# One tile of the weights' ring for the key and value rows of the window branch, in a one-core decoder layer on Trainium2

## Chip, cores and metric

The kernel runs on one core of one Trainium2 chip. The metric is the time of one execution in microseconds (us), by the median of repeated runs. Five engines have queues of their own: TensorE (PE, with its weight loads PEld), VectorE (DVE), ScalarE (ACT), GpSimd (POOL) and SyncE (SP). SP, ACT and POOL also issue the transfers between device memory and on-chip memory (DMAs). A name that ends in q, such as ACTq, is the sequencer of that engine when it issues a DMA.

## The reference

One layer of a decoder for 512 new prompt positions and 8 single new tokens, all in float32. The input projection has the columns of a state space group (u), of the queries, of three key and value branches (compressed, selected, sliding window) and of the gates:

```
proj = jnp.dot(h, lp['w_in'])
u, q, k_c, v_c, k_s, v_s, k_w, v_w, g = jnp.split(proj, offsets, axis=-1)
...
gates = jax.nn.sigmoid(g.astype(jnp.float32)).reshape(bsz, t, 3, N_HEADS)
o_ssm, s_last = ssm_mixer(u, ssm_s0, lp)
o_attn, win_state = attend(q, gates, kv_cmp, kv_slc, kv_win)
mix = jnp.concatenate([rmsnorm(o_ssm, ...), rmsnorm(o_attn, ...)], axis=-1)
x = x + gt1[:, None, :] * jnp.dot(mix, lp['w_out'])
...
x = x + gt2[:, None, :] * jnp.dot(jnp.square(jax.nn.relu(jnp.dot(h2, lp['w_up']))), lp['w_down'])
```

The key and value rows of the new positions (kv_cmp, kv_slc, kv_win) are outputs of their own.

## The kernel before, in words

Activations lie with the 1024 features on the partitions (8 blocks of 128) and 520 tokens along a row (512 prompt positions and 8 samples). Every float32 product is made of three matmuls: `split` (L65 to L67) makes a rounded copy on ACT (`wH` of weights, `hH` of activations) and the remainder on DVE (`wL`, `hL`), and the products hH·wH, hL·wH and hH·wL are added up in PSUM.

Weights come by DMA into `rawt(...)` tiles: one ring named `raw` of three buffers, 128 x 2048 float32 (1 MB) each, taken in turn by all weight loads of the layer (`wkv`, `wq`, `wglu` and others). A buffer can be filled again when the splits that read it are done.

`kv_proj(c)` does branch c (0 compressed, 1 selected, 2 window). It loads `wkv`, splits it in two halves, and goes over five token tiles t: four of 128 prompt positions and one of the 8 samples. A tile has 24 matmuls into a PSUM tile `pkv` (tag `pj`, two buffers; L660). For c of 1 and 2 ACT then copies the keys, each group twice, to `kvt` (L688) and the values to `Vx` (L690), stores both from ACT's own queue (L691 for the keys, L692 for the values), and PE transposes `kvt` into `pkt` (L695), from which `split` makes `KH` and `KL`. For c of 2 the gates come from the same PSUM tile (L117 on ACT, L118 on DVE). For t = 4 ACT copies `kvs` (L663). `kvt` is a tile of its own with two buffers, so that tile t takes the buffer of tile t - 2.

Behind each of the two `kv_proj` calls for c = 1 and 2 stands `state_space_outputs` for one of four feature blocks q (here q = 0 and 1): eight DMAs `yc`, four from SP and four from POOL (L903), bring scan results back from the scratch `yscr`, DVE adds them to `yf` (L905, L908) and `gelu` follows (`zt`, `uT`). `yc` has one buffer: the DMAs of block q wait for the `yf` of block q - 1. The next loop, for s = 0 and 1, loads 1 MB of query weights `wq` (L917), splits them (`wH<-wq`, `wL<-wq`), projects the queries with the matmuls `pj` (L619), and does blocks 2 and 3. Later loads of interest are three or four `rwin` (window rows of the samples, 1 MB each, L1165) and `wglu` (L1279).

The order on each engine isn't the order of the code: a scheduler with a simulated time line (`schedule_with_timeline_sim=True`) sets it, with waits on semaphores where tiles pass between engines. A DMA that SP or ACT issues gets one of eight completion semaphores (`DMAHW0` to `DMAHW7`), handed out in turn over the program, and before it is issued its engine waits for the DMA that had that semaphore before it. DMAs of POOL have eight of their own (`DMASW0` to `DMASW7`).

Of the kernel before, what the change touches and what calls it, by code (L numbers as in the profile page):

```python
# [10 lines left out]
F32 = mybir.dt.float32  # L11
# [6 lines left out]
P = 128  # L18
# [19 lines left out]
def body(tc, i, o, dbg=None):  # L38
# [19 lines left out]
    def pst(tag, name):  # L58
        if tag in bank.get("turns", ()):
            tag = next(bank["turns"][tag])  # L60
        return bank["tile"].tile([P, 512], F32, tag=tag, name=name, bufs=bank["tags"][tag])
# [3 lines left out]
    def split(h, l, src):  # L65
        nc.scalar.copy(h, src)  # L66
        nc.vector.tensor_tensor(l, src, h, ALU.subtract)  # L67
# [3 lines left out]
    def rawt(name):  # L71
        return raw.tile([P, 2048], F32, tag="raw", name=name)
# [42 lines left out]
    def sigmoid_(dst, src):  # L115

        nc.scalar.activation(dst, src, AF.Tanh, scale=0.5)  # L117
        nc.vector.tensor_scalar(dst, dst, 0.5, 0.5, op0=ALU.mult, op1=ALU.add)  # L118
# [61 lines left out]
    def whl(a, b):  # L180
        h = wp.tile([P, 1120], F32R, tag="wH", name="wH", bufs=2)[:, : a * b].rearrange("p (a b) -> p a b", a=a)
        l = wp.tile([P, 1120], F32R, tag="wL", name="wL", bufs=2)[:, : a * b].rearrange("p (a b) -> p a b", a=a)
        return h, l
# [422 lines left out]
    p1 = p1x.enter_context(tc.tile_pool(name="p1", bufs=1, side="right", reuse_waits="tile"))  # L606
# [30 lines left out]
    def kv_proj(c):  # L637
        c0 = 1024 + 256 * c
        r = rawt("wkv").rearrange("p (k c) -> p k c", k=KT)
        nc.sync.dma_start(r, i["w_in"][0, :, c0 : c0 + 256].rearrange("(k p) c -> p k c", p=P))  # L640
        nw = 280 if c == 2 else 256
        if c == 2:
            rg = p1.tile([P, KT, 24], F32, name="rg")
            nc.sync.dma_start(rg, i["w_in"][0, :, 1792:1816].rearrange("(k p) c -> p k c", p=P))
        ws = []
        for kk in range(2):
            kr = slice(4 * kk, 4 * kk + 4)
            h, l = whl(4, nw)
            split(h[:, :, 0:256], l[:, :, 0:256], r[:, kr])
            if c == 2:  # L650
                split(h[:, :, 256:280], l[:, :, 256:280], rg[:, kr])
            ws.append((h, l))
        for t in range(5):
            tok = slice(t * P, t * P + (P if t < 4 else NB))
            mp = P if t < 4 else NB
            ps = pst("pj", "pkv")
            for k in range(KT):
                wh, wl = ws[k // 4]
                for n, (x, w) in enumerate(((hH, wh), (hH, wl), (hL, wh))):
                    nc.tensor.matmul(ps[0:mp, 0:nw], x[:, k, tok], w[:, k % 4], start=(k == 0 and n == 0),  # L660
                                     stop=(k == KT - 1 and n == 2))
            if t == 4:
                nc.scalar.copy(kvs[:, c * 256 : (c + 1) * 256], ps[0:NB, 0:256])  # L663
                if c < 2:
                    nc.scalar.dma_start(o["new_%s_sample" % onames[c]], kvs[:, c * 256 : (c + 1) * 256])
                else:
                    nc.scalar.dma_start(o["new_win_sample"][:, T - 1], kvs[:, 512:768])
            else:
                kvt = p1.tile([P, 256], F32, tag="kvt", name="kvt", bufs=2)
                out = o["new_%s_prompt" % onames[c]][tok]  # L670
                if c == 0:
                    nc.scalar.copy(kvt, ps[:, 0:256])
                    nc.scalar.dma_start(out, kvt)
                    pk = pst("tr", "pkc")
                    for n in range(2):
                        nc.tensor.transpose(pk[:, n * P : (n + 1) * P], kvt[:, n * P : (n + 1) * P], ident)
                    for g in range(2):
                        for j2 in range(2):
                            for n in range(2):
                                nc.vector.tensor_copy(  # L680
                                    xTp[j2 * 64 : j2 * 64 + 64, n, g, :, t * 8 : t * 8 + 8],
                                    pk[g * 64 : g * 64 + 64, n * P : (n + 1) * P].rearrange(
                                        "p (c jp j2) -> p j2 jp c", c=8, j2=2)[:, j2])
                else:
                    br = c - 1

                    kv2 = kvt.rearrange("p (g a d) -> p g a d", g=2, a=2)
                    nc.scalar.copy(kv2, ps[:, 0:P].rearrange("p (g d) -> p g d", g=2).unsqueeze(2).to_broadcast([P, 2, 2, HD]))  # L688
                    vt = Vx[:, t, 2 * br : 2 * br + 2]
                    nc.scalar.copy(vt, ps[:, P:256].rearrange("p (g d) -> p g d", g=2))  # L690
                    nc.scalar.dma_start(out[:, 0:P].rearrange("t (g d) -> t g d", g=2), kv2[:, :, 0])  # L691
                    nc.scalar.dma_start(out[:, P:256].rearrange("t (g d) -> t g d", g=2), vt)  # L692
                    pk = pst("tr", "pkt")
                    for g in range(2):
                        nc.tensor.transpose(pk[:, g * P : (g + 1) * P], kvt[:, g * P : (g + 1) * P], ident)  # L695
                    split(KH[:, 2 * br : 2 * br + 2, tok], KL[:, 2 * br : 2 * br + 2, tok],
                          pk[:, 0:256].rearrange("p (g t) -> p g t", g=2))
            if c == 2:
                sigmoid_(gates[0:mp, t], ps[0:mp, 256:280])
    kv_proj(0)  # L700
    ada(4, "ad")

# [37 lines left out]
    for qd in range(NG // GQ):  # L740
# [89 lines left out]
        for g in range(GQ):  # L830
            c = slice(g * 80, (g + 1) * 80)
# [80 lines left out]
    for c in (1, 2):  # L912
        kv_proj(c)
        state_space_outputs((c - 1,))
# [715 lines left out]
```

## Time and profile before

| | |
|---|---|
| timed runs | 898.96, 900.66, 900.21 us, median 900.21 us |
| the profiled execution | 896.71 us, with a span of 895.0 us |
| granted TensorE clock, mean | 0.987 of full speed |
| PE busy | 845.8 us, 94% |
| PEld, DVE, ACT, POOL busy | 751.8, 519.8, 389.9, 64.0 us |

The span goes from the first to the last instruction that the profiler recorded; 1.7 us of the execution lie outside it. All rows below are from this one execution. Times of rows count from the start of the span.

### The profile page before, as it was taken

Reading aid. Unit: us, or ns where it says so; the run is one execution under the profiler, and the core shown is the slowest. Engines: PE = TensorE matmul, PEld = TensorE weight load, DVE = VectorE, ACT = ScalarE, POOL = GpSimd, SP = SyncE. Lnnn points to the kernel's source line nnn. Section 1 sums busy time; section 2 is a strip of 40 time slices with the busy share of each in tenths; the row PEclk is TensorE's granted clock in tenths of the full one; section 3 lists DMA queues with packets and bytes.
Section 4 is the critical chain, followed back from the end, with each engine's and each line's share of the span. In section 5 each row is a group of like instructions: output and inputs, shape, how many; then the busy total and the mean of one; then the engine's idle time right before and its main releaser. Section 6 shows DMA issues by size and latency. Waiting matters only on the chain.

```text
span 895.0 us, 16400 instructions
## 1 busy us (share of the span) xinstructions
PE 845.8 (94%) x6527; PEld 751.8 (84%) x6527; DVE 519.8 (58%) x1365; ACT 389.9 (44%) x883; POOL 64.0 (7%) x147
## 2 busy tenths in 40 slices
PE   2799998999998999998989999999999999999996
PEld 1557997888987766756679989999999999999996
DVE  5876666785766466668667874442333444434533
ACT  1555317453435466556655554442111344433322
POOL 6001201000152100000000000000000000000000
PEclk9999998999999999999989999999999999999998
DMA  8957577473773441203266553333333333232302
GB/s 290 319 195 247 181 157 193 138 247 116 203 244 92 165 166 64 77 2 142 73 210 198 180 190 94 94 96 94 95 95 95 94 95 92 82 86 75 92 1 96
DMA packets 111836, 122.36 MB, mean 137 GB/s; under 512 B 24500, under 2 KB 91880, under 8 KB 109584
## 3 DMA queue, kind: packets, MB, share of 16 engines
q1 hardware_dynamic: 101968, 88.66, 32.8%
q0 software_dynamic: 5488, 29.99, 9.6%
q10 hardware_dynamic: 4304, 2.66, 1.1%
q8 instruction: 51, 0.84, 0.4%
q14 instruction: 25, 0.20, 0.1%
HBM read 112.47 MB, written 13.03 MB: 140 GB/s over the span
## 4 chain that ended last, share of the span: by engine, by line
PE 66%; DVE 2%; ACT 1%; issue 0%; ACTq 0%; DVEq 0%
PE pup L1427 21%; PE pdn L1427 21%; PE pwo L1427 5%; PE pj L619 3%; PE po L1268 2%; PE ptp L1261 2%; PE pg L1289 2%; PE pS L1047 2%; PE pst L1232 1%; PE pkT L1038 1%; PE pst L1233 1%; PE psc L1174 1%; PE pstat L879 1%; PE poS L1136 0%; PE po L1349 0%; PE pst L1234 0%
## 5 line engine op out<-in xcount | busy, mean ns | idle before, releaser
L1427 PE MATMUL pdn<-hidH,wL 128*128 128x256 f32 (+1 forms) x480 | 136.0, 283 | 0.0
L1427 PE MATMUL pdn<-hidL,wH 128*128 128x256 f32 (+1 forms) x480 | 135.8, 283 | 0.0
L1427 PE MATMUL pup<-h2L,wH 128*128 128x256 f32 (+1 forms) x480 | 135.5, 283 | 0.0
L1427 PE MATMUL pdn<-hidH,wH 128*128 128x256 f32 (+1 forms) x480 | 135.3, 282 | 0.0
L1427 PE MATMUL pup<-h2H,wL 128*128 128x256 f32 (+1 forms) x480 | 135.0, 282 | 0.0
L1427 PE MATMUL pup<-h2H,wH 128*128 128x256 f32 (+1 forms) x480 | 134.5, 283 | 0.0
L1427 PEld LDWEIGHTS pup<-h2L,wH 128*128 128x128 f32 x480 | 90.4, 188 | 0.8 <-DVE rs L105 0.8
L1427 PEld LDWEIGHTS pup<-h2H,wH 128*128 128x128 f32 x480 | 89.8, 188 | 0.8 <-ACT h2H L66 0.8
L1427 PEld LDWEIGHTS pdn<-hidH,wL 128*128 128x128 f32 x480 | 90.4, 188 | 0.0
L1427 PEld LDWEIGHTS pdn<-hidL,wH 128*128 128x128 f32 x480 | 90.2, 188 | 0.1
L1427 PEld LDWEIGHTS pup<-h2H,wL 128*128 128x128 f32 x480 | 90.3, 188 | 0.0
L1427 PEld LDWEIGHTS pdn<-hidH,wH 128*128 128x128 f32 x480 | 90.3, 188 | 0.0
L66 ACT CAST wH<-wdn 128x1024 fp32r<-128x1024 f32 x30 | 31.5, 1049 | 114.2 <-PE pdn L1427 104.3
L67 DVE TENSOR_TENSOR wL<-wup,wH 128x1024 fp32r<-128x1024 f32 x30 | 36.7, 1225 | 57.9 <-ACT wH L66 57.9
L67 DVE TENSOR_TENSOR wL<-wdn,wH 128x1024 fp32r<-128x1024 f32 x30 | 36.8, 1225 | 54.3 <-ACT wH L66 54.3
L401 PE MATMUL ph<-xc,w 128*128 128x256 f32 (+2 forms) x320 | 62.9, 346 | 0.7 <-DVE xc L391 0.7
L401 PEld LDWEIGHTS ph<-xc,w 128*128 128x128 f32 x320 | 50.8, 194 | 11.0 <-issue 5.4
L66 ACT CAST wH<-wup 128x1024 fp32r<-128x1024 f32 x30 | 31.5, 1050 | 47.3 <-PE pup L1427 37.5
L1507 ACT ACTIVATE rl<-pup 128x256 f32<-128x256 f32 (+1 forms) x64 | 24.5, 385 | 45.5 <-PE pup L1427 45.4
L389 ACT COPY xc<-pxc 64x256 f32<-64x256 f32 x96 | 32.1, 366 | 22.5 <-DVE xc L391 18.8
L1508 DVE TENSOR_TENSOR rl<-rl 128x256 f32<-128x256 f32 (+1 forms) x64 | 27.2, 426 | 22.9 <-ACT rl L1507 22.9
L1436 DVE SCALAR_TENSOR_TENSOR xT<-pdn,mod,xT 128x256 f32<-128x256 f32 x32 | 15.2, 478 | 41.7 <-PE pdn L1427 41.6
(569 smaller groups left out, 2038.8 us busy)
## 6 DMA issues: line engine op xcount, KB each, us to landing
wada<-w_ada SPq DMA_DIRECT2D x20, 1024.0 KB, 5.1
wup<-w_up SPq DMA_DIRECT2D x16, 1024.0 KB, 5.4
wdn<-w_down SPq DMA_DIRECT2D x16, 1024.0 KB, 5.7
wo<-w_out SPq DMA_DIRECT2D x8, 1024.0 KB, 5.5
wada<-w_ada SPq DMA_DIRECT2D x8, 512.0 KB, 16.0
rwin<-state_win SPq DMA_DIRECT2D x4, 1024.0 KB
new_win_sample<-state_win POOLq DMA_DIRECT2D x2, 2044.0 KB, 8.6
wkv<-w_in SPq DMA_DIRECT2D x3, 1024.0 KB, 8.1
```

Of the source, the lines that this page charges most:

```text
L66: nc.scalar.copy(h, src)
L67: nc.vector.tensor_tensor(l, src, h, ALU.subtract)
L389: nc.scalar.copy(dst[:, :, :, hf], srcv[:, :, :, hf])
L401: nc.tensor.matmul(phv[:, lo:hi, 0:w], w1[n][:, r_], xc[n][:, lo:hi, r_ % 8, off : off + w], start=(r_ == 0), stop=(r_ == 15))
L619: nc.tensor.matmul(ps[:, 0:HB], w[:, k], x[:, k, hc], start=(k == 0 and n == 0), stop=(k == KT - 1 and n == 2))
L1047: nc.tensor.matmul(S[b4 * 32 : b4 * 32 + 32], q4[:, 4 * grp + b4], kts[b4], start=True, stop=True)
L1261: nc.tensor.transpose(pt_[:, c : c + P], at(qt, kt * P, P), ident)
L1268: mm = nc.tensor.matmul(po[hh * 64 : hh * 64 + 64, kt * P : T], Vx[:, kt, kb], PT[:, c0 : c0 + T - kt * P], start=(br == 0 and kt == 0), s ...
L1289: nc.tensor.matmul(ps[:, 0:HB], r[:, k, c], zf[k][:, hc], start=(k == 0), stop=(k == 3))
L1427: nc.tensor.matmul(ps[:, 0 : b - a], w, x[:, a:b], start=first and n == 0, stop=last and n == 2)
L1507: nc.scalar.activation(rl, ps[:, 0 : b - a], AF.Relu)
L1508: nc.vector.tensor_tensor(rl, rl, rl, ALU.mult)
```

## The change

For the window branch (c = 2) `kv_proj` takes one more tile of the weights' ring, `kvr`, behind the splits of the weights, and token tile t uses its columns 256t to 256t + 255 as `kvt`. For the other branches nothing changes. From here on a line of the code stands two lines lower (L688 becomes L690, L691 and L692 become L693 and L694, L903 becomes L905, L917 becomes L919).

```diff
@@ -650,6 +650,8 @@
             if c == 2:
                 split(h[:, :, 256:280], l[:, :, 256:280], rg[:, kr])
             ws.append((h, l))
+
+        kvr = rawt("kvt") if c == 2 else None
         for t in range(5):
             tok = slice(t * P, t * P + (P if t < 4 else NB))
             mp = P if t < 4 else NB
@@ -666,7 +668,7 @@
                 else:
                     nc.scalar.dma_start(o["new_win_sample"][:, T - 1], kvs[:, 512:768])
             else:
-                kvt = p1.tile([P, 256], F32, tag="kvt", name="kvt", bufs=2)
+                kvt = kvr[:, t * 256 : (t + 1) * 256] if c == 2 else p1.tile([P, 256], F32, tag="kvt", name="kvt", bufs=2)
                 out = o["new_%s_prompt" % onames[c]][tok]
                 if c == 0:
                     nc.scalar.copy(kvt, ps[:, 0:256])
```

The ring then goes round in the order wkv (c = 1), wkv (c = 2), kvr, wq, wq, wglu instead of wkv, wkv, wq, wq, wglu. The second `wq` so takes the buffer of the second `wkv`, where it took that of the first, and `wglu` takes that of `kvr`. The scheduler also sets another order in several places.

On ACT, in the window branch, these were the rows from the copy of tile 2 to the first cast of query weights. In brackets is what an instruction waits for; `Activation` and `PE` are those engines.

```order
L688 COPY kvt<-pkv 128x256 [waits DMAHW1_49,PE_49]
L690 COPY Vx<-pkv 128x128
L117 ACTIVATE gates<-pkv 128x24
L691 DMA new_win_prompt<-kvt 128x2x64 [waits DMAHW0_49,Activation_49]
L692 DMA new_win_prompt<-Vx 128x128 [waits Activation_49]
L688 COPY kvt<-pkv 128x256 [waits DMAHW3_49,PE_49]
L690 COPY Vx<-pkv 128x128
L117 ACTIVATE gates<-pkv 128x24
L66 CAST KH<-pkt 128x2x128 [waits PE_49]
L691 DMA new_win_prompt<-kvt 128x2x64 [waits DMAHW2_49,Activation_49]
L692 DMA new_win_prompt<-Vx 128x128 [waits DMAHW4_49,Activation_49]
L66 CAST wH<-wq 128x1024 [waits PE_49]
```

In the changed kernel this stands on ACT from the second store of tile 1 to the first store of tile 3; the second store of tile 3 (L694) and the cast `wH<-wq` are the next two rows.

```order
L694 DMA new_win_prompt<-Vx 128x128 [waits DMAHW7_49,Activation_49]
L690 COPY kvt<-pkv 128x256 [waits PE_49]
L692 COPY Vx<-pkv 128x128
L117 ACTIVATE gates<-pkv 128x24
L66 CAST KH<-pkt 128x2x128 [waits PE_49]
L693 DMA new_win_prompt<-kvt 128x2x64 [waits DMAHW0_49,Activation_49]
L694 DMA new_win_prompt<-Vx 128x128 [waits DMAHW1_49,Activation_49]
L66 CAST KH<-pkt 128x2x128 [waits PE_49]
L690 COPY kvt<-pkv 128x256 [waits PE_49]
L692 COPY Vx<-pkv 128x128
L117 ACTIVATE gates<-pkv 128x24
L693 DMA new_win_prompt<-kvt 128x2x64 [waits DMAHW3_49,Activation_49]
```

The two copies `kvt` lost their waits for a DMA; before, those were the stores of tiles 0 and 1. The second store of tile 1 and the first store of tile 2 now wait for the semaphores 7 and 0, which by the turn of the program were last given to the two `wq` loads.

On SP, at the place where the selected branch begins, these were the rows (`mscr`, `Tz` and `yscr` belong to the state space scan):

```order
L785 DMA mscr<-M_2385 128x64 [waits DVE_49]
L835 DMA yscr<-ys 128x320 [waits DMAHW3_49,Activation_49]
L917 DMA wq<-w_in 128x8x256 [waits DMAHW4_49,PE_49]
L917 DMA wq<-w_in 128x8x256 [waits DMAHW6_49,PE_49]
L787 DMA Tz<-mscr 128x8x64 [waits DMAHW7_49,DMAHW2_49]
L785 DMA mscr<-M_2487 128x64 [waits DVE_49]
```

In the changed kernel SP has the `wq` loads behind the last `yscr` and the first `yc` of block 3:

```order
L837 DMA yscr<-ys 128x320 [waits DMAHW5_49,Activation_49]
L905 DMA yc<-yscr 16x8x80 [waits DMAHW0_49,DMAHW1_49,DMASW5_49,DMAHW2_49,DMASW4_49,DMAHW3_49,DMASW3_49,DMAHW6_49,DMASW2_49,DVE_49]
L919 DMA wq<-w_in 128x8x256 [waits DMAHW7_49]
L919 DMA wq<-w_in 128x8x256
L905 DMA yc<-yscr 16x8x80
L905 DMA yc<-yscr 16x8x80 [waits DMAHW5_49,DMAHW4_49]
L905 DMA yc<-yscr 16x8x80
L1167 DMA rwin<-state_win 128x2x1024 [waits DMAHW2_49,PE_49]
L1167 DMA rwin<-state_win 128x2x1024 [waits DMASW3_49,DMASW6_49,DMASW2_49,DMASW7_49,DMASW1_49,DMAHW4_49,DMASW0_49,PE_49]
L1167 DMA rwin<-state_win 128x2x1024 [waits DMAHW6_49]
L1281 DMA wglu<-ssm_w_glu 128x4x512 [waits DMAHW1_49,DMAHW0_49,DMAHW3_49,PE_49,Activation_49]
```

The two loads of the query weights moved behind thirteen `yc`, both `Tz` and all `yscr`, and are issued once the `yf` of block 2 is done, for which the `yc` ahead of them waits. `wglu`, which stood ahead of the `rwin` loads, now stands behind three of them.

## Rows read from the trace of the kernel before

**Rows 1.** Page, busy time of each engine and its share of the span.

```profile
PE 845.8 (94%) x6527; PEld 751.8 (84%) x6527; DVE 519.8 (58%) x1365; ACT 389.9 (44%) x883; POOL 64.0 (7%) x147
```

**Rows 2.** Waits, 252 to 280 us: who waits for whom, total, times, longest.

```profile
ACT kvt L688 <- DMA new_win_prompt<-kvt: 6.2, 2, 3.4
...
PE pj L619 <- ACT wH L66: 1.3, 1, 1.3
...
PE pkt L695 <- ACT kvt L688: 1.1, 2, 0.7
...
PE pkv L660 <- DVE wL L67: 0.5, 1, 0.5
```

**Rows 3.** Timeline of ACT, window branch: start, duration, instruction, idle time before it.

```profile
259.13 0.39 ACTq L691 DMA_DIRECT2D new_win_prompt<-kvt  x1
...
266.68 0.37 ACT L688 COPY kvt<-pkv 128x256 f32<-128x256 f32 x1 [2.87 <-DMA new_win_prompt<-kvt]
...
267.08 0.39 ACTq L691 DMA_DIRECT2D new_win_prompt<-kvt  x1
...
267.51 0.48 ACTq L692 DMA_DIRECT2D new_win_prompt<-Vx  x1
270.67 0.37 ACT L688 COPY kvt<-pkv 128x256 f32<-128x256 f32 x1 [3.35 <-DMA new_win_prompt<-kvt]
```

**Rows 4.** Timeline of PE, window branch to the first query projection.

```profile
252.52 0.32 PE L660 MATMUL pkv<-wH,hL 128*8 128x256 f32 x1
...
266.48 0.29 PE L660 MATMUL pkv<-wH,hL 128*128 128x280 f32 x1
267.11 0.44 PE L695 MATMUL pkt<-ident,kvt 128*128 128x128 f32 x2 [0.34 <-ACT kvt L688]
...
270.06 0.29 PE L660 MATMUL pkv<-wH,hH 128*8 128x280 f32 x1
...
273.12 0.39 PE L619 MATMUL pj<-hH,wH 128*128 128x260 f32 x1 [1.33 <-ACT wH L66]
...
274.73 0.42 PE L619 MATMUL pj<-hH,wL 128*128 128x260 f32 x1
...
277.98 0.30 PE L619 MATMUL pj<-hH,wL 128*128 128x260 f32 x1
278.12 0.28 PE L619 MATMUL pj<-hH,wH 128*128 128x260 f32 x1
...
278.60 0.28 PE L619 MATMUL pj<-hL,wH 128*128 128x260 f32 x1
```

**Rows 5.** Windows: stretch, length, engines' busy time (instructions), granted clock, DMA share, GB/s.

```profile
234.00:239.00 5.00, 5.00 (x45) 5.00 (x44) 1.82 (x7) 1.39 (x5) 0.16 (x2) 1.00 1.16 319
275.00:278.00 3.00, 3.00 (x16) 3.00 (x16) 2.85 (x5) 0.78 (x2) 0.91 (x1) 0.50 0.03 7
410.00:420.00 10.00, 8.40 (x52) 5.46 (x52) 8.88 (x24) 8.08 (x24) 0.00 (x0) 1.00 0.56 227
450.00:470.00 20.00, 18.23 (x117) 15.87 (x116) 12.33 (x39) 11.04 (x25) 0.00 (x0) 0.83 0.55 188
```

**Rows 6.** Timeline of SP: the query weights, and the loads in the window branch.

```profile
226.93 1.76 SPq L917 DMA_DIRECT2D wq<-w_in  x2
...
256.46 2.89 SPq L1165 DMA_DIRECT2D rwin<-state_win  x3
270.67 1.96 SPq L903 DMA_DIRECT2D yc<-yscr  x4
```

**Rows 7.** Timeline of ACT, selected branch.

```profile
238.58 0.35 ACTq L692 DMA_DIRECT2D new_slc_prompt<-Vx  x1
238.97 0.37 ACT L66 CAST KH<-pkt 128x256 fp32r<-128x256 f32 x1 [3.59 <-DMA wq<-w_in]
```

**Rows 8.** Timeline of DVE, window branch.

```profile
256.74 0.70 DVE L127 TENSOR_TENSOR uT<-zt,yf 128x520 f32<-128x520 f32 x1
...
267.75 1.12 DVE L905 SCALAR_TENSOR_TENSOR yf<-uT,vec,yc 128x512 f32<-128x512 f32 x1 [0.22 <-DMA new_win_prompt<-Vx]
```

**Rows 9.** Page, DMA issues: times, KB each, median us from issue to landing.

```profile
wup<-w_up SPq DMA_DIRECT2D x16, 1024.0 KB, 5.4
...
wada<-w_ada SPq DMA_DIRECT2D x8, 512.0 KB, 16.0
```

## The prediction, made before the result was known

> **What bounds the kernel now.** I read the busy times first: PE works 94% of the span [rows 1], so a change can save only where PE stands still or runs slowly, and what it saves there reaches the end if PE stays the bound behind it. Then I looked at the waits of the stretch that the diff touches. Three of them are PE's and hang together: PE waits 1.1 us in two pieces for the copies `kvt`, and 1.3 us for the cast of the first query weights, while ACT itself waits 6.2 us in two pieces for the stores of earlier `kvt` tiles; 0.5 us more PE waits for the second split of the window weights [rows 2]. The timeline of ACT gives the reason. The store of tile 0 is issued at 259.13, and the copy of tile 2, which takes its buffer, starts at 266.68; that of tile 3 starts at 270.67, 3.35 us of it waiting for the store of tile 1 [rows 3]. Both stores are 64 KB and lie in flight beside `rwin` loads of 1 MB each, issued from 256.46 [rows 6]. On PE the reader is to see that matmuls run without a gap until 266.48, and that the first query matmul stands at 273.12 [rows 4]. Last I read the granted clock: from 275 to 278 it is 0.50, the 1.2 GHz level, although PE is busy all the time there [rows 5]. It fell behind this cluster of gaps and came back at 278.
>
> What lies between is counted so. At 266.48 PE still has one matmul under way (0.13 us), then a pair of transposes, 24 matmuls and another pair. From 267.11 to 270.06 the first pair and 22 matmuls take 2.95 us to the start of the last of them [rows 4]; one of the steps is 0.13 us, so the whole rest is 2.95 + 3 x 0.13 + 0.26 = 3.6 us. It could end at 266.61 + 3.6 = 270.2, and the query matmuls begin 2.9 us later than that. Behind them come 15 matmuls from 274.73 to 277.98, 0.217 us apart; from 278.12 to 278.60 four steps take 0.12 us each [rows 4]. The low clock costs 15 x (0.217 - 0.12) = 1.4 us.
>
> **The change part by part.** *The buffers.* Four `kvt` tiles get four places, so the two waits of ACT for stores, 2.87 and 3.35 us [rows 3], are gone from the program; the rows of ACT in the new order show the copies waiting for PE alone. Without any other wait PE would reach the query matmuls at 270.2 instead of 273.12, and 0.47 us earlier still if the wait for the second split went too: 269.7.
>
> *The loads of the query weights.* In the old order SP issues both `wq` at 226.93 [rows 6], 40 us ahead of need. In the new one they stand behind the `yf` of block 2. I place that so: on DVE the `uT` ahead of it ends at 256.74 + 0.70 = 257.4 in the old order, and a `yf` takes 1.12 us and a short second part, 0.2 [rows 8], which makes 258.7. That chain begins with the copy of the samples' rows on ACT, which needs the matmul at 252.52; before, this matmul stood behind the seven small scan products, and now it stands ahead of them, which gives it up to 0.9 us. So the `yf` ends at 257.8. One `yc` of 1.96/4 = 0.5 us is issued first [rows 6], so that the first `wq` is issued at 258.3.
>
> The trace has no load of `wq` under these conditions. Its nearest row for one load of the same size and shape is `wup`, 5.4 us from issue to landing [rows 9]. For the second I add the time to move 1.05 MB at the 319 GB/s that ran when the old `wq` loads ended [rows 5]: 3.3 us. The second lands at 258.3 + 5.4 + 3.3 = 267.0. The bounds are 265.3 (`yf` 0.7 us earlier and a rate of 410 in place of 319, which saves 0.7 more, and a little off the first) and, above, the row of eight queued `wada` loads, 16.0 us from issue to landing [rows 9]: 274.3.
>
> *The new wait.* ACT's first store of tile 2 waits for the semaphore that the second `wq` holds. Behind it in ACT's queue stand one more store, a cast `KH`, the copies of tile 3 with gates, two stores and the cast `wH<-wq`, and PE's last transposes and all query matmuls wait for these. Their time from the rows: stores 0.39 and 0.48 [rows 3], a cast 0.37 [rows 7], and from the copy of tile 3 to the first query matmul 273.12 - 270.67 = 2.45 [rows 3, 4]; together 3.7 us. With the second `wq` at 267.0 the query matmuls begin at 270.7, and 269.7 is their floor. The gain up to there is 273.12 - 270.7 = 2.4 us. Each us by which `wq` is later costs one; at 273.12 - 3.7 = 269.4 nothing is left.
>
> That ACT can be held so, the trace shows already: in the selected branch a store waited 3.59 us for a `wq` load and was issued at 238.58 [rows 7]. There nothing of it reached PE, which was busy 5.00 of the 5 us [rows 5]. That wait goes, since the loads moved; it was covered and gives nothing.
>
> *The clock.* The cluster of three gaps before 274 shrinks to one of about 1 us ahead of the query matmuls, and the short ones for `wL` and `kvs` behind it, which stay. Elsewhere PE was busy 8.40 of 10 us at a clock of 1.00, from 410 to 420 [rows 5], while 18.23 of 20 us from 450 to 470 went with 0.83 [rows 5]. So gaps of such a size decide it either way. I take the clock as kept: 1.4 us gained; the other bound is nothing.
>
> *What else moves.* On POOL, the `yc` of block 2 now stand ahead of the stores of the scan's states, which nobody in the kernel reads. `rwin` comes up to 4 us later, and its first reader is 40 us away. In the attention stage, 400 to 470 us, products are ordered anew. I find no term there that points one way; the stretch 450 to 470 has 1.8 us of idle PE [rows 5], and I take this as the size of what a new order can give or take, with nothing in the middle.
>
> **Sum.** 2.4 + 1.4 + 0 = 3.8 us. The profiled execution of 896.71 us becomes 892.9, and its span of 895.0 becomes 891.2. The median of the timed runs lies 3.5 us above the profiled execution; from it the same gain makes 900.2 - 3.8 = **896.4 us**. About 0.2%, 1.8 us, is what a measurement of this kernel can tell from no change.
>
> **What speaks against it.** The store of tile 0, 64 KB, needed 7.5 us from issue until its buffer was taken again, and that of tile 1 some 10 us [rows 3], beside the three `rwin` loads [rows 6]. The Trainium skill, page "DMA: Bandwidth & Descriptors", section "Queues, rings and completion order", says that a DMA engine takes turns between the queues that have work for it, and that the write which signals completion lands only behind all earlier writes of that engine, over all its queues. The stores of the trace agree with the second half, at 7.5 us for 64 KB. By that rule the `wq` signal would come behind whatever small stores and `yc` transfers went ahead, so somewhat later than my sum has it, and the stores of tiles 0, for which tiles 2 and 3 wait too, would come with it.
>
> **Rivals.**
>
> *The wait only changes its name.* ACT waits for `wq` as long as it waited for the stores. For it: the first `wq` goes out 1.8 us later than the first `rwin` did before [rows 6], and two `rwin` follow closely. Against it: 2 MB stand ahead of the signal, where the store that held tile 3 had three `rwin` of 1 MB ahead of it [rows 3, 6]. It takes a second `wq` at 268.5 to 270.5, a gain of 0.9 to a loss of 1.1, with the clock falling as before: 899.3 to 901.3, say 900.2.
>
> *Slower.* The same wait, but with the two `rwin` loads taking their share of the engines before `wq` is complete. 4.2 MB at the 319 GB/s of the old `wq` loads [rows 5] take 13.2 us, and 2.1 us of start (5.4 less 3.3) come ahead of it: the second `wq` lands at 258.3 + 15.3 = 273.6, near the 16.0 us of the `wada` row. The query matmuls begin at 277.3, and the time is 900.2 + 4.2 = 904.4. It decides for slower from a `wq` at 269.4 + 1.8 = 271.2. Against it: all these loads come from SP, in this order. The same page of the Trainium skill speaks of turns between queues, not between loads of one queue, and has descriptors of one queue consumed in order; no run so far shows the two loads apart.
>
> *Half the gain.* The copies come early, but the clock falls all the same, or the new order of the attention stage takes back 1.8 us: 2.4 us of gain in the first case, 2.0 in the second, 898.
>
> That the change doesn't do what it says can be left out, since the order shows the copies without their waits.
>
> **How the numbers follow.** The forecast, a gain of 3 to 5.5 us (up to 3.4 at the floor of 269.7, 1.4 of the clock, and a little of the attention stage), has 0.48: 894.7 to 897.2 is its own range. Half the gain 0.18, the wait that changes its name 0.22, slower 0.12. Faster by over 0.2%, so below 898.4, is the forecast and most of half the gain: 0.65. Within 0.2% is the third case with the rest: 0.23. Slower is 0.12. The range has to leave out no more than 2 in 10: from 894.4, a little below the forecast's own, to 901.0, which leaves out the slower case and the top of the third.
>
> **What the profile of the changed kernel would show.** Right: no copy `kvt` of the window branch waits for a DMA; ACT's first store of tile 2 is issued near 267, released by `wq`; PE begins the query matmuls near 270.7 with one gap of about 1 us ahead; the granted clock stays at 1.00 from 270 to 280; all later stages are shifted by the same 3 to 4 us. Wrong, if the first `wq` is issued much behind 258.3 (the `yf` of block 2 late), if its landing takes over 11 us (the other two cases), if the clock row of 275 to 278 comes back, or if PE's idle time between 400 and 470 us grows from what it was by over 1.8 us.

## The result: 893.8 us, and where it lies in the profile after

The changed kernel took 894.54, 893.93, 893.70 and 892.50 us, median 893.82 us. The kernel before, with one more run beside it, has a median of 899.59 us. The ratio is 0.9934, with a 95% interval of 0.9916 to 0.9952: faster by 5.8 us, where 3.8 us were forecast, and 0.6 us below the range. Of the runs further down one of e9, 1375.5 us at a mean clock of 0.563, is left out of its median.

The profiled execution of the changed kernel took 894.54 us, so that the two profiled executions differ by 2.2 us only. This is the first thing to understand, and most of the runs below serve it. The page of the changed kernel, span and busy times of the engines (for [rows 1]):

```profile
span 892.8 us, 16399 instructions
...
PE 847.5 (95%) x6527; PEld 753.3 (84%) x6527; DVE 521.7 (58%) x1365; ACT 389.8 (44%) x883; POOL 64.8 (7%) x147
```

Its waits from 252 to 280 us, in the form of [rows 2]:

```profile
ACT kvt L690 <- DMA wq<-w_in: 2.6, 1, 2.6
...
PE pj L619 <- ACT wH L66: 1.2, 1, 1.2
...
PE pj L619 <- DVE wL L67: 0.2, 1, 0.2
```

The waits for stores are gone, PE's two waits for `kvt` and the one ahead of the second split too. What is left is one wait of PE for the cast of the query weights, and one of ACT for a `wq` load. It reads as a wait of the copy `kvt`; the timeline of ACT shows that it is the store ahead of it (for [rows 3]):

```profile
261.09 0.39 ACTq L693 DMA_DIRECT2D new_win_prompt<-kvt  x1
...
264.03 0.34 ACTq L694 DMA_DIRECT2D new_win_prompt<-Vx  x1
264.41 0.37 ACT L690 COPY kvt<-pkv 128x256 f32<-128x256 f32 x1 [2.57 <-DMA wq<-w_in]
...
264.92 0.39 ACT L66 CAST KH<-pkt 128x256 fp32r<-128x256 f32 x1
267.73 0.39 ACTq L693 DMA_DIRECT2D new_win_prompt<-kvt  x1
...
268.95 0.38 ACT L690 COPY kvt<-pkv 128x256 f32<-128x256 f32 x1
...
270.43 1.04 ACT L66 CAST wH<-wq 128x1024 fp32r<-128x1024 f32 x1 [0.84 <-PE pkt L697]
```

The second store of tile 1 is issued at 264.03 and the first store of tile 2 at 267.73, each after a stop of ACT's sequencer: by the order these two wait for the two `wq` loads. SP issued those at 257.01 (for [rows 6]):

```profile
257.01 1.74 SPq L919 DMA_DIRECT2D wq<-w_in  x2
258.80 2.49 SPq L905 DMA_DIRECT2D yc<-yscr  x3
267.91 1.59 SPq L1167 DMA_DIRECT2D rwin<-state_win  x3
```

On PE the window branch begins at 253.35 and the query products at 271.52, against 252.68 (the table below) and 273.12 [rows 4]. So this execution came 0.7 us later to the branch, and took 18.17 us from its first product to the first query product, before 20.44.

```profile
253.35 0.51 PE L662 MATMUL pkv<-wH,hH 128*128 128x280 f32 x2
...
271.52 0.39 PE L619 MATMUL pj<-hH,wH 128*128 128x260 f32 x1 [1.20 <-ACT wH L66]
```

The windows behind (for the second of [rows 5]; columns as there) show the clock down here too, for about as long, only earlier:

```profile
271.00:275.00 4.00, 3.30 (x16) 2.95 (x17) 3.72 (x9) 2.55 (x6) 0.71 (x1) 0.75 1.04 405
275.00:278.00 3.00, 3.00 (x21) 3.00 (x21) 0.79 (x3) 0.73 (x3) 0.34 (x1) 0.76 1.06 407
```

### The profile page after: what moved, and what is told of

Its sections match the earlier page's. It is cut to its first block, busy times and chain, and to the rows that moved or that the text cites. A ratio compares the mean times of both kernels' runs of the same rounds, so it can differ in the third digit from the quotient of the medians.

```text
span 892.8 us, 16399 instructions
## 1 busy us (share of the span) xinstructions
PE 847.5 (95%) x6527; PEld 753.3 (84%) x6527; DVE 521.7 (58%) x1365; ACT 389.8 (44%) x883; POOL 64.8 (7%) x147
## 4 chain that ended last, share of the span: by engine, by line
PE 62%; issue 4%; DMA 2%; ACT 1%; DVE 1%; ACTq 0%; DVEq 0%; POOLq 0%
PE pup L1429 21%; PE pdn L1429 21%; PE pwo L1429 5%; PE pj L619 3%; PE pg L1291 2%; PE ptp L1263 1%; PE po L1270 1%; DMA xT<-xscr 1%; PE pS L1049 1%; PE pst L1234 1%; PE pkT L1040 1%; PE pst L1235 1%; PE psc L1176 1%; PE pstat L881 1%; PE poS L1138 0%
## 5 line engine op out<-in xcount | busy, mean ns | idle before, releaser
L1244 ACT ACTIVATE pe<-pst,mxa 128x512 f32<-128x512 f32 (+1 forms) x64 | 33.4, 529 | 16.9 <-DVE mxa L1240 15.5
```

What stands on the lines that cost most here:

```text
L1244: nc.scalar.activation(at(qt, 0, nk), d, AF.Exp, bias=mx[:, qt : qt + 1], accum_out=dn[:, qt : qt + 1])
```

## Experiments

**More traces of both kernels** (no edit). Executions of one kernel differ here by up to 7 us, so one pair of traces says little of 5 us.

e1, the kernel before in five rounds:

> The kernel before, unchanged, to learn how its executions differ. The timed runs moved by 5.8 us, the two profiled executions only by 2.2 us. Theory A: the first profiled execution of before (896.7 us) was a short one and the usual one is near 899.6, with one more stretch at half clock or a longer one somewhere; then this ratio is 1.000 within 0.002, the times lie at 898 to 901, and a second trace shows half-clock stretches that add up to 1 to 3 us more than before's. Theory B: the timed runs of before were the odd ones; then this one lies at 896 to 897.5.

e2, the changed kernel in five rounds:

> The changed kernel, unchanged. Theory A: a ratio of 0.993 to 0.995 again, 893 to 895 us. Theory B: 0.997, 896 to 897. In both the query projection begins 2.4 us earlier against the start of the window branch than before, with ACT's first store of tile 2 released by the second load of query weights.

Measured: e1 had 898.94 us (895.87 to 902.41), a ratio to the kernel before of 0.9995 [0.9976, 1.0013]; e2 had 894.47 (893.15 to 896.18), 0.9934 [0.9913, 0.9955]. Theory A holds for the times: the first profiled execution of before, 896.71, was a short one. The trace of e1 has one more fall of the clock than the first, 3.4 us long, from 37 to 41 us, long before the window branch.

Then single executions, for traces:

> The kernel before once more, for a trace of a usual execution: the runs of it so far lie at 895.7 to 902.4 with mean clocks of 0.987 to 0.981, and both traces in hand are from the better end (0.987 and 0.985). If the timed gain of 5 to 6 us, beyond the 2.9 us that the stages show, is a matter of the clock, a trace at 0.983 or 0.981 shows one or two more half-clock stretches than the first, each costing about 1.5 us, and the same waits. If it isn't, such a trace shows a longer wait or transfer somewhere.

> As e6: one more execution of the kernel before. The stretch from the window branch's first product to the first query product takes 20.4 to 20.9 us whatever the clock does elsewhere; what differs from trace to trace is the number and place of half-clock stretches.

> The changed kernel once more: 18.0 to 18.2 us from the window branch's first product to the first query product, and one half-clock stretch of 3.4 us behind it. If the changed kernel has fewer half-clock stretches as a rule, its mean clock is 0.985 to 0.987 again where before's are 0.981 to 0.985.

> One more execution of the kernel before, for a trace with a mean clock of 0.983 or less, as 29 of 56 runs of it had. If the usual execution differs from the traces in hand by the clock alone, its waits and its stretch of 20.4 to 20.9 us are the same, and it has one or two half-clock stretches more, each 3.4 us long and worth about 1.6 us.

> The kernel before once more, like the run ahead of it: a trace with a mean clock of 0.983 or less is wanted. Its waits in the window branch and its stretch of 20.4 to 20.9 us should be the same, with one or two half-clock stretches of 3.4 us more than in the first trace.

> The kernel before once more. From the window branch's first product to the end the six traces of it take 641.9 to 642.9 us, three traces of the changed kernel 639.2 to 639.5. If the rest of the timed gain (5.1 us of medians against 2.9 us of this) comes from chance ahead of the window branch, the start of that branch here is anywhere from 252.5 to 257 and the part behind it 642 to 643 again. If before has executions in which the part behind is longer (a second half-clock stretch in the window branch or in the attention stage), it is 644 or more in some of these looks.

> The kernel before once more, with the two theories of the run ahead of it: the part behind the window branch's first product takes 642 to 643 us in every execution and the rest is the time ahead of it, or it takes 644 us or more in some of them, with a half-clock stretch that the first traces lack.

> The changed kernel once more. Chance ahead of the window branch: that branch starts at 252.5 to 257 as in before, and 639 to 640 us follow. If the two kernels differ ahead of it, though their instructions are the same up to 225 us, the start stays at 253 to 255 in all looks at the changed kernel while before's goes to 256 or more.

> The changed kernel once more, with the theories of the run ahead of it: a start of the window branch anywhere from 252.5 to 257 and 639 to 640 us behind it, or a start that stays at 253 to 255.

The table has, for each execution with a trace, the start of the window branch (first product with 280 columns), the time from there to the first query product, from there to the first `psc` (the product behind the first half of the query products), from there to the end of the span, the mean granted clock and the time. All in us, from the timelines of PE.

| execution | start | to queries | to psc | rest | clock | time |
|---|---|---|---|---|---|---|
| before, first | 252.68 | 20.44 | 14.21 | 607.7 | 0.987 | 896.71 |
| e1 | 254.12 | 20.93 | 14.16 | 607.4 | 0.985 | 898.33 |
| e6 | 253.01 | 20.47 | 14.05 | 607.4 | 0.987 | 896.58 |
| e7 | 254.27 | 20.58 | 14.17 | 607.5 | 0.985 | 898.21 |
| e12 | 253.66 | 21.39 | 12.67 | 608.3 | 0.985 | 897.73 |
| e13 | 256.84 | 21.23 | 14.18 | 607.5 | 0.983 | 901.37 |
| e14 | 254.65 | 21.06 | 12.67 | 608.4 | 0.983 | 898.52 |
| e15 | 253.79 | 21.15 | 15.47 | 608.8 | 0.982 | 900.91 |
| changed, first | 253.35 | 18.17 | 14.00 | 607.3 | 0.985 | 894.54 |
| e2 | 255.00 | 17.98 | 14.02 | 607.5 | 0.985 | 896.18 |
| e8 | 252.88 | 18.20 | 12.47 | 608.5 | 0.987 | 893.80 |
| e16 | 253.98 | 18.06 | 12.47 | 608.4 | 0.985 | 894.62 |
| e17 | 254.59 | 17.98 | 12.48 | 608.0 | 0.985 | 894.85 |

The means are 20.91, 13.95 and 607.9 before, 18.08, 13.09 and 607.9 after: 2.8 us of stall, 0.9 us in the query products, nothing in the rest. To the query products the two kernels don't overlap. Not all of the expectations held: four of before's executions took longer than the expected 20.4 to 20.9 us to the query products, and e8 lacks the low clock that was expected behind them. From the start of the branch to the end of the span e15 took 645.4 us, the sign of the second theory of e14 and e15; the other seven of before took 641.9 to 642.9, the five of the changed kernel 638.5 to 639.5.

The second column goes with the clock: e8, e16 and e17 kept it. The windows of e8 that answer to those shown above:

```profile
271.00:275.00 4.00, 3.75 (x27) 3.39 (x28) 3.88 (x8) 2.11 (x6) 1.05 (x1) 1.00 1.04 408
275.00:278.00 3.00, 3.00 (x28) 3.00 (x27) 1.95 (x5) 2.06 (x6) 0.00 (x0) 1.00 1.08 403
```

But of the 1.5 us that the clock gives back there about 0.9 are taken again later. Wherever the query products kept the clock, in e8, e16 and e17 as in e12 and e14 of before, the clock fell at 408 to 420, in the attention stage, and the rest took 608.0 to 608.5 us; in seven of the other eight it didn't fall there, and the rest took 607.3 to 607.7. The same window in the first trace of the changed kernel and then in e8:

```profile
405.00:420.00 15.00, 12.18 (x76) 8.10 (x76) 14.23 (x37) 9.76 (x27) 1.25 (x2) 1.00 0.55 210
...
405.00:420.00 15.00, 12.56 (x60) 8.90 (x60) 12.51 (x32) 11.09 (x31) 0.00 (x0) 0.77 0.45 179
```

The other end is e15, an execution of the kernel before in which the branch and the query products take 36.6 us, against 30.5 in e17. Its windows:

```profile
254.00:258.00 4.00, 3.41 (x16) 3.33 (x16) 3.93 (x9) 2.31 (x5) 4.00 (x7) 0.63 0.50 132
...
275.00:282.00 7.00, 6.45 (x30) 6.22 (x31) 4.67 (x8) 2.80 (x7) 1.05 (x1) 0.54 0.28 53
```

Here the clock fell twice: at 254, around the wait for the second split of the window weights, 0.59 us in this trace, and again behind the gaps at 275, for twice as long as in the first trace. All eight traces of before have the low clock somewhere in this stretch, of the changed kernel two of five. Added up over windows of 1 us from the start of the branch to 480 us, the time at 1.2 GHz is 10.1 to 10.2 us in all five traces of the changed kernel and in five of before; e12 and e14 have 13.6 and e15 20.3. What these three have more begins with a fall at 254 or 255, behind PE's wait for the second split, a wait that the changed kernel lacks. So the falls differ from execution to execution; that the changed kernel has fewer of them here rests on three traces of eight against none of five.

The start of the branch differs by up to 4.2 us between executions of before, with the low clock more or less often ahead of it; the means, 254.1 before and 254.0 after, are the same, as they should be with the same order of instructions up to about 225 us.

**e3: four buffers, loads early.** Before, with four buffers from a small pool for the window branch:

```diff
-                kvt = p1.tile([P, 256], F32, tag="kvt", name="kvt", bufs=2)
+                kvt = kw.tile([P, 256], F32, tag="kvw", name="kvt", bufs=4) if c == 2 else p1.tile([P, 256], F32, tag="kvt", name="kvt", bufs=2)
...
+    kwx = ExitStack()
+    kw = kwx.enter_context(tc.tile_pool(name="kw", bufs=1, reuse_waits="tile"))
     for c in (1, 2):
...
```

> Before, with four buffers for kvt in the window branch from a pool of its own; the ring keeps its old order, so the query weights are loaded early as before. If the gain comes from the buffers alone, the copies of tiles 2 and 3 follow PE, the query matmuls begin near 270.0 (before 273.1, changed kernel 271.5 or 270.7 when its later start is taken off), and the time is 1 us or more below the changed kernel's. If ACT's stores then wait for other loads (wglu and rwin stand on the semaphores), the first store of tile 2 waits until about 262 to 265 and costs nothing that PE sees. If the gain came from the new order of other work and not from the buffers, the ratio stays within 0.998 to 1.002.

Measured: 898.13 us, ratio 0.9990 [0.9972, 1.0007]. In its trace the branch took 17.44 us and the stretch to `psc` 12.23 us with the clock up, together 5.0 us less than in the first trace of before and 5.2 less than the mean, as the buffers' theory has it. The rest took 615.5 us in place of 607.9: the scheduler had put the attention stage in another order, and the clock fell there. This execution, 902.62 us, was the slowest of the twelve of e3, so that the loss in the rest is probably smaller in most of them. Windows of e3 and then of the kernel before:

```profile
300.00:340.00 40.00, 37.90 (x234) 24.77 (x233) 26.37 (x92) 22.65 (x68) 4.03 (x17) 0.91 0.43 159
```

```profile
300.00:340.00 40.00, 38.50 (x267) 26.28 (x265) 27.52 (x99) 23.10 (x66) 4.03 (x17) 1.00 0.44 159
```

The time alone would have spoken against the buffers; the stage speaks for them.

**e10: two buffers and two.** As e3, but only tiles 2 and 3 in the pool, with two buffers, which leaves the attention stage nearly in the changed kernel's order:

```diff
+                kvt = kw.tile([P, 256], F32, tag="kvw", name="kvt", bufs=2) if c == 2 and t > 1 else p1.tile([P, 256], F32, tag="kvt", name="kvt", bufs=2)
...
```

> Before, with tiles 2 and 3 of the window branch in two more buffers of a small pool: four buffers in all, the ring and the early loads of the query weights as before, and an attention stage in nearly the order of the changed kernel. If the buffers are the gain and the late loads a cost, the window branch's first product to the first query product takes 17.4 us as in e3 (before 20.4 to 20.9, changed kernel 18.0 to 18.2), the clock stays up behind it and the next stretch takes 12.2 instead of 14.0 to 14.2, and the later stages are as in the changed kernel: a gain of 5 us of the stages, so 1.5 to 2.5 us less than the changed kernel: 891.5 to 893 us, ratio 0.991 to 0.992. If the late loads are what helps (a later wq leaves the memory to others), this kernel stays at or above the changed kernel's 894.

Measured: 893.99 us (892.69 to 895.80), ratio 0.9935 [0.9911, 0.9959]. The branch took 17.30 us and the stretch behind it 12.42: as expected, 0.8 us less than the changed kernel in the first, and the clock up. Its waits in the window branch:

```profile
ACT kvt L688 <- PE pkv L660: 5.2, 3, 3.3
...
PE pkv L660 <- DVE wL L67: 0.3, 1, 0.3
...
PE pkn L1007 <- ACT kvs L663: 0.2, 1, 0.2
```

No copy waits for a transfer, and PE's only wait ahead of the query products is 0.3 us for the second split. The time was expected 1.5 to 2.5 us below the changed kernel's and isn't: 893.99 and 894.47 can't be told apart. In its trace the rest took 609.2, 1.3 us more than the changed kernel's mean. So four buffers, without the ring and with the query weights early, give all of the gain, and the branch is 0.8 us shorter than with the late loads, which didn't show in the end. In this trace the clock fell both at 408 and at 459.

One thing moved with the buffers, in e3 too: the scheduler has the three `rwin` behind the branch, so that the stores have only `wglu` in flight beside them, where before had `wglu` and three `rwin`.

```profile
272.51 1.52 SPq L1168 DMA_DIRECT2D rwin<-state_win  x3
```

How much of the 3.6 us between before's mean and this comes from that, e3 and e10 can't tell. e11, below, has the three `rwin` beside the stores and four places.

**e9: late loads only.** Two buffers as before, and the query weights in a pool of their own (opened as in e3), for which the scheduler moves `wglu` early and `wq` late:

```diff
-        r = rawt("wq").rearrange("p (k c) -> p k c", k=KT)
+        r = kw.tile([P, 2048], F32, tag="wqr", name="wq", bufs=2).rearrange("p (k c) -> p k c", k=KT)
...
```

> Before, with two buffers for kvt as before, and the query weights in a pool of their own (wglu now comes early and the wq loads come late, behind the last yscr). It has the later loads without the four buffers. If the four buffers make the gain, the copies of tiles 2 and 3 wait for the stores of tiles 0 and 1 as before, now beside two wq loads in place of wglu and rwin: 6 us of waits of ACT, the first query product 20 us or more behind the window branch's first, and no gain: 898 to 902. If the late loads make the gain (the stores of tiles 0 and 1 land sooner with less ahead of them), that stretch is 18 to 19 us long and the time falls by 2 us or more, as far as the attention stage stays as it was.

Measured: 898.45 us, ratio 0.9996 [0.9980, 1.0011]; the branch took 18.95 us: neither theory as it stood. ACT waits for the stores as long as before, but once instead of twice:

```profile
260.86 0.39 ACTq L691 DMA_DIRECT2D new_win_prompt<-kvt  x1
...
269.00 0.37 ACT L688 COPY kvt<-pkv 128x256 f32<-128x256 f32 x1 [5.99 <-DMA new_win_prompt<-Vx]
...
270.62 0.38 ACT L688 COPY kvt<-pkv 128x256 f32<-128x256 f32 x1
```

Two `wq` of 1 MB are in flight here in place of `wglu` and three `rwin`. The store of tile 0 still takes 8.1 us from its issue to the copy of tile 2, but that of tile 1 has landed by the time the copy of tile 3 comes, which waits for no store. By this one trace, and against e10's 17.30 us, two buffers cost 3.6 us in before's mean and 1.7 here: with two buffers, about half of the stall hangs on what lies beside the stores. The rest took 611.8 us, again in another order of the attention stage, and took the gain back.

**e11: later still.** The changed kernel with only tiles 2 and 3 in the ring's tile; the scheduler puts `wq` behind three `rwin`:

```diff
-                kvt = kvr[:, t * 256 : (t + 1) * 256] if c == 2 else p1.tile([P, 256], F32, tag="kvt", name="kvt", bufs=2)
+                kvt = kvr[:, t * 256 : (t + 1) * 256] if c == 2 and t > 1 else p1.tile([P, 256], F32, tag="kvt", name="kvt", bufs=2)
```

> The changed kernel with only tiles 2 and 3 in the ring's tile. The scheduler then puts both wq loads behind three rwin loads, and no store of ACT waits for wq, only the first cast of the query weights does. With 3 MB of rwin ahead at 0.4 MB per us the first wq lands 6 to 8 us later than in the changed kernel, at 269 to 272 after a start of the window branch at 253. If the place of wq in SP's queue sets the query products, they begin 20 to 22 us behind the window branch's first product (changed kernel 18.1), and the half-clock stretch comes back. If SP's loads share the engines evenly, wq lands with the last rwin, and it is 23 us or more. The attention stage has another order here too, so the time itself, 897 to 903, tells less than the stage.

Measured: 906.21 us, ratio 1.0079 [1.0048, 1.011], above the expected 897 to 903. The copies of tiles 2 and 3 wait for PE alone, though three `rwin` are issued beside the stores:

```profile
258.78 1.95 SPq L1167 DMA_DIRECT2D rwin<-state_win  x3
```

```profile
263.77 0.38 ACT L690 COPY kvt<-pkv 128x256 f32<-128x256 f32 x1
...
266.61 0.37 ACT L690 COPY kvt<-pkv 128x256 f32<-128x256 f32 x1 [2.20 <-PE pkv L662]
```

They start 10.65 and 13.49 us after the branch, before 14.00 and 17.99. So the four places take the waits for stores away, with three `rwin` beside the stores too. SP issued the `wq` loads at 265.06, and ACT and PE waited for them:

```profile
273.93 1.99 ACT L66 CAST wH<-wq 128x1024 fp32r<-128x1024 f32 x2 [2.92 <-DMA wq<-w_in]
```

```profile
275.03 0.48 PE L619 MATMUL pj<-hH,wH 128*128 128x260 f32 x1 [3.83 <-ACT wH L66]
```

The cast begins 273.93 - 253.12 = 20.8 us after the start of the branch, in the changed kernel 270.43 - 253.35 = 17.1; the query products begin 21.91 and 18.17 us after it. A cast 3.7 us later makes the query products 3.7 us later: one for one. The place of `wq` in SP's queue set it, as the first theory had it, though the first load landed after 272; the second theory's 23 us or more didn't come, and the clock fell behind the gap, from 275 to 279. The rest, 613.6 us, adds to it.

**e5: stores on POOL.** The changed kernel with the window branch's stores issued by POOL:

```diff
-                    nc.scalar.dma_start(out[:, 0:P].rearrange("t (g d) -> t g d", g=2), kv2[:, :, 0])
-                    nc.scalar.dma_start(out[:, P:256].rearrange("t (g d) -> t g d", g=2), vt)
+                    eng = nc.gpsimd if c == 2 else nc.scalar
+                    eng.dma_start(out[:, 0:P].rearrange("t (g d) -> t g d", g=2), kv2[:, :, 0])
+                    eng.dma_start(out[:, P:256].rearrange("t (g d) -> t g d", g=2), vt)
```

> The changed kernel with the stores of the window branch's key and value rows issued by POOL, so that no wait of such a store stands in ACT's queue. If the wait of ACT's stores for the query loads is what is left of the stall (1.2 us of PE idle ahead of the query matmuls), the first cast wH of the query weights runs near 268 when its load has landed, the query matmuls begin about 1 us earlier than in the changed kernel, and the half-clock stretch behind them may go: 1 to 2.5 us less than the changed kernel. If the load's landing itself is the limit, or POOL is late with yc, the time is the changed kernel's within 0.5 us.

Measured: 901.02 us, ratio 1.0026 [1.0007, 1.0044], 6.6 us slower than the changed kernel beside it. The first half is right: with no store in ACT's queue the query products begin 16.81 us after the branch. Two of them later PE stops for 2 us:

```profile
272.73 0.22 PE L1007 MATMUL pkn<-ident,kvs 8*128 8x8 f32 x1 [1.98 <-ACT kvs L665]
```

`kvs` stands in ACT's queue behind a `zt` that waits for DVE's `yf`, which the scheduler had moved ahead. So the stretch to `psc` took 14.00 us with the clock at 1.00, the stall was moved and not removed, and the rest took 613.9 us.

## Why the prediction came out as it did

**Bound and place: right.** PE's waits for `kvt` and the wait for the second split went, as in the first part of the prediction.

**The late loads and the new wait: right, to half a us.** The second `wq` was forecast at 267.0 and released the store at 267.73 in an execution that was 0.7 us late, so 267.06. Two errors inside cancel, which is luck: the first `wq` was issued at 257.01, less 0.7 is 256.3, 2.0 us earlier than forecast, and the pair took 10.7 us from there, forecast 8.7. From the signal to the first query product it took 271.52 - 267.73 = 3.8 us, forecast 3.7. The query products were forecast at 270.7, and came at 271.52 - 0.67 = 270.85. The gain up to there, forecast 2.4 us, is 2.3 in the first pair of traces and 2.8 in the means. e11 shows the last link of the price of one us for each us, from the cast to the products; no run makes the second `wq` alone later. `rwin`, forecast up to 4 us later, came 10.8 later (267.91 less 0.67, against 256.46), since SP waited 6.6 us for a `yc` transfer ahead of it.

**The clock's term and the base: the step that failed.** The prediction read one fall of the clock in one execution, put it down to the gaps ahead of the query products, took its 1.4 us as gone and bounded what the change could give back by nothing and these 1.4 us. The runs show something else. In the first pair of traces it gave 0.2. Over the executions the low clock isn't gone from behind the branch: the changed kernel has it for 10.1 to 10.2 us up to 480 in all five traces, part of them behind the query products or else from 408 on. What before has more comes in some executions only, begins at the wait for the second split, and isn't one number: 3.4 us at the low clock in e12 and e14, 10.1 in e15. From the start of the branch to `psc` before took from 33.7 us (e14) to 36.6 (e15), the changed kernel from 30.5 (e17) to 32.2 (its first), so that two executions differ there by 1.6 to 6.2 us; by the means it is 0.9 us of clock and not 1.4.

The base was mis-sized too. 900.21, the median of three runs, lies 1.1 us above the 899.12 of 72 runs. From 899.12 the same 3.8 us make 895.3, and the range that ended at a gain of 5.8 us (900.2 less 894.4) would have reached down to 893.3, which holds the measured 893.8. With the clock's bounds from several executions the low end would have stood lower still.

**The sum against the timed runs: partly open.** By the means of the traces the stretch gives 2.8 + 0.9 = 3.7 us and the whole executions 898.5 - 894.8 = 3.7 us, which is the forecast of 3.8. That the sum fits is in part luck: the stall gave more than its 2.4 us and the clock less than its 1.4. The medians of all runs differ by more, 899.12 (72 runs, 895.1 to 902.4, mean clock 0.984) and 894.21 (13 runs, 892.5 to 896.2, 0.986): 4.9 us. Runs of the same clock differ by less: at 0.985 the medians are 898.3 and 894.8, at 0.987 896.6 and 893.8, so 3.5 and 2.8 us. What the medians have beyond goes with the number of falls of the clock: a mean clock of 0.983 or less have 40 of the 72 runs of before and none of the 13 of the changed kernel. That is too much for chance in the draw of the runs. Where in the kernel these falls lie, the traces show only in part: three of before's eight have more of them behind the start of the branch, and ahead of it both kernels have 6.8 to 13.6 us of low clock, 8.9 on average before and 9.5 after.

**The attention stage: right on average, lucky in kind.** Nothing was forecast for the new order and the rest took 607.9 us in both, and among executions with the same falls of the clock the means of the two kernels agree to 0.1 us. But in e3, e5, e9 and e11 the rest is 4 to 8 us longer, in four of the five other kernels tried, by one trace each (e3's of its slowest run). The 1.8 us that the prediction allowed for it was too small a bound.

**The rivals.** The wait did change its name, ACT now waits for `wq`, but 1.4 us of PE's waiting is left of 2.9. The slower case needed the second `wq` 4 us later; e11 is near that case in another kernel. Its mechanism, two `rwin` that share the engines with `wq`, wasn't put to the test: SP issued `rwin` at 267.91, when both `wq` had signalled. Half the gain, 898, is what the first pair of traces shows, 2.2 us, and not what the runs show.

From the real issue of the first `wq`, at 256.3 on the scale of the first trace, the forecast's transfer times make 265.0 for the second; its signal came at 267.06, 2.1 us later. Most of that is the first load: its signal came 7.0 us after its issue, at 264.03, forecast 5.4. The lateness has the direction of the rule of the Trainium skill that the prediction set against itself, page "DMA: Bandwidth & Descriptors", section "Queues, rings and completion order": a completion signal comes behind all earlier writes of its engine, over all queues. The trace agrees in sign, with `yc` transfers and stores in flight beside; no run here separates the signal from the data. That tiles 2 and 3 would wait for the stores of tile 0, as the prediction adds there, is a slip: their copies wait for PE alone.

## What to carry to other kernels

Too few buffers for a tile that is stored cost more here where big loads were in flight beside the stores; before adding buffers, ask what is in flight when the store is issued (e9: the same two buffers, half the stall). Where a scheduler orders the program, judge an edit by the stage that it touches and by the rest apart: e3 removed the whole stall and lost most of it again in the attention stage. A fall of the clock that goes in one place can come in another: add up the low clock over the stages behind before counting it as gained. And take the base of a forecast, and the cost of the clock, from several executions where runs of one kernel differ by more than the gain.

## What the runs showed of the hardware that was not expected

The granted clock in one place of one program differs between its executions: e8, e16 and e17 kept 2.4 GHz behind the gaps at the query products, and two other executions of the same kernel fell to 1.2 GHz. Of these e2 and e17 have the same two waits of PE, 1.01 us for the cast and 0.17 for the remainder; e2 fell and e17 didn't. Of the kernel before, runs at a mean clock of 0.987, 0.985, 0.983 and 0.981 had medians of 896.6, 898.3, 899.4 and 901.3 us: most of the spread of its runs goes with this.

In e5 some instructions of DVE and of POOL that ran beside each other between 269 and 277 us took longer than elsewhere. The `yf` of 512 columns took 1.58 us where it took 1.12 before [rows 8], and the first of these two rows of POOL stands beside it; the second stands beside rows of DVE of the usual length. The first of their forms took 0.93 us in the kernel before, the second 0.19:

```profile
269.64 1.78 POOL L968 TENSOR_SCALAR_AFFINE_SELECT gsum<-gsum 64x256 f32<-64x256 f32 x1
...
274.48 2.25 POOL L981 TENSOR_SCALAR_AFFINE_SELECT mapa<-mapa 64x16 f32<-64x16 f32 x1
```

The Trainium skill, page "GPSIMD Engine Reference", section "Specifications", has POOL share its memory interface with DVE, with contention from DVE instructions that read two tensors there. `yf` is one; the trace agrees, and no run here took the two apart.
